# Grouping the small score products of two attentions, summing squares four tiles at a time, and a new order

## The chip, the core and the metric

The kernel runs on one core of a Trainium2 chip. A core has TensorE (PE, matrix products; its weight loads, PEld, overlap them), VectorE (DVE), ScalarE (ACT), GpSimd (POOL), the queue of SyncE (SP) that starts the transfers, and 16 DMA engines. Each engine works through its own instruction list in the order in which it was written. The metric is the device time of one execution in microseconds (us), here the median of timed runs; the profile shows one execution.

## The reference, cut to what matters

256 tokens of width 1024, in float32, with 16 learned meta tokens put ahead of them (T = 272 rows), go through four layers. Shortened:

```python
# layer 0 and 1, each: h = h + rmsnorm(mix(rmsnorm(h))); h = h + rmsnorm(conv_ffn(rmsnorm(h)))
# mix of layer 0, forgetting attention, 16 heads of 64
s = einsum('bhqd,bhkd->bhqk', q, k) * scale + c_q[..., :, None] - c_k[..., None, :]
o = softmax(where(causal, s, NEG)) @ v * sigmoid(og)
# mix of layer 1, gated DeltaNet, 8 heads of 128
dec = exp(where(incl, gc[..., :, None] - gc[..., None, :], -inf))
A, qk = (k @ k.T) * dec * beta, (q @ k.T) * dec
...
# conv_ffn
gate, up = split(causal_dwconv(h @ w_up, conv_w)); return (gelu(gate) * up) @ w_down
# then, without the meta tokens: MLA (16 heads), layer_norm, MoBA (16 heads of 64), layer_norm
```

With 256 tokens and blocks of 256, MoBA has one block, so it is causal attention with rotated queries and keys, times silu of a gate.

## The kernel before, in words

**A recorder and a planner.** The kernel is written once in program order, but nothing is emitted at once: `Rec.add` records each operation, with an estimated cost from `_cost` and the operations it depends on, under the name of a part (`ameta`, `att3`, `dout0`, `bq2`). Operations inside a `bundle` become one entry and stay together. `Rec.order` then plays the engines against each other: it always takes the operation that can start first, and between those that can start together the one with the lowest rank, which is the place in program order minus numbers of the table `SHIFT` for the part and for the part on one engine. It models PE's clock (`PeClock`), the DMA of the weights (three constants) and the places in the buffer pools. Where it foresees a gap of PE of 400 ns or more, `keep_warm` fills it with products of a mask that nobody reads (tile `idle`, line L449). All other instructions are issued from one line, L498, so the profile tells them apart by tile names.

**Weights.** Each MB of weights comes as one fp32 tile `raw` through SP's queue into one of two buffers; ACT writes its rounded part `wh`, DVE the rest `wl`, and PE adds three products per tile of 128 rows: `wh` with `xh`, `wl` with `xh`, `wh` with `xl`. Activations lie transposed, as tiles of 128 features by up to 272 tokens. The accumulators are PSUM banks: tag `psm` for projections, at most 5 at a time, `psx` for everything else, at most 6.

**Norms.** `rstd` (L914) multiplies each square tile `sq` by a full 128x128 matrix of ones (`const` in the rows) into one bank, so that every row of the bank holds the sum over features, and `ln_exp` makes `rstd` of it. `sq_rstd` (L922) does so for the 6 tiles of MLA's query latent; `pre` (L931), the norm ahead of a projection, for 8 tiles, one at a time, as each residual tile becomes ready.

**Scores of the forgetting attention.** `attend` (L1108) treats the 256 tokens; the 16 meta tokens as queries are treated in `meta` (L1158): per head a 16x16 block gets the score product (`km`, `qm`), the decay of the keys (one row of the table `crow`, picked by a one-hot column `oh`) and the causal mask (`causb` times the unit matrix `identb`).

**DeltaNet.** `dn_scores` (L1374) runs four times, for the keys and the queries of two groups of four heads. It adds mask and decay into one bank (`pe`) and the product into another (`pk`); first for the 16 meta rows of four heads, then for two blocks of 128 tokens per head. The code is, for the second:

```python
for c in range(2):
    with nc.bundle():
        nc.tensor.matmul(pe[:, s], self.identb, mask, start=True, stop=False)
        nc.tensor.matmul(pe[:, s], oh[:, h:h + 1].to_broadcast([96, P]), rows[:, a:b], start=False, stop=True)
        nc.tensor.matmul(pk[:, s], k[:, 4 * g + h, a:b], x[:, 4 * g + h, a:b], start=True, stop=True)
```

**A product in column strips.** `narrow` (L866), the projection to 16 gate logits, multiplies four weight tiles of 32 columns into four strips of 32 rows of one bank, in one bundle.

**MoBA.** `rope64` (L1702) makes the rotated queries `bq` of two heads from a projection through ACT copies and three DVE operations; `causal_pairs` (L1647) multiplies them with the keys `bk`, 2 heads and 2 query blocks at a time, four products in one bundle.

## Time and profile before

| | |
|---|---|
| timed runs | 1137.41, 1146.93, 1147.97 us; median 1146.93 |
| profiled execution | 1139.0 us, its span 1137.2 |
| mean granted clock of PE | 0.989 |
| busy, of the span | PE 96%, PEld 91%, DVE 73%, ACT 60%, POOL 1% |
| DMA | 159.05 MB, mean 140 GB/s |
| instructions | PE 9064 products, DVE 1847, ACT 1372 |

PE's busy time counts overlapping products once, and a product's row carries the time from its start until its result is out, so neighbours overlap: the distance of two starts is what one costs PE. A row "a <- b, c" names the tile written and the tiles read. "x2" behind an fp32 product of small tiles is one product in two passes.

### The profile page before, as it was taken

Reading aid. Unit: us, or ns where it says so; the run is one execution under the profiler, and the core shown is the slowest. Engines: PE = TensorE matmul, PEld = TensorE weight load, DVE = VectorE, ACT = ScalarE, POOL = GpSimd, SP = SyncE. Lnnn points to the kernel's source line nnn. Section 1 sums busy time; section 2 is a strip of 40 time slices with the busy share of each in tenths; the row PEclk is TensorE's granted clock in tenths of the full one; section 3 lists DMA queues with packets and bytes.
Section 4 is the critical chain, followed back from the end, with each engine's and each line's share of the span. In section 5 each row is a group of like instructions: output and inputs, shape, how many; then the busy total and the mean of one; then the engine's idle time right before and its main releaser. Section 6 shows DMA issues by size and latency. Waiting matters only on the chain.

```text
span 1137.2 us, 22513 instructions
## 1 busy us (share of the span) xinstructions
PE 1095.8 (96%) x9064; PEld 1031.4 (91%) x9064; DVE 828.8 (73%) x1847; ACT 684.5 (60%) x1372; POOL 10.3 (1%) x85
## 2 busy tenths in 40 slices
PE   7999999999999989999999999999999999999897
PEld 6998889899999978888889899999989988999887
DVE  5678774798876577899755789986475667856686
ACT  4567655665655465554686656565355589556881
POOL 0000000000000000000000000000000000000000
PEclk9999989999999999999999999999999999999999
DMA  7552323354645543234122345655545452466331
GB/s 222 169 161 82 112 75 112 112 189 153 198 157 169 177 148 112 75 112 140 49 75 75 112 149 193 204 188 189 175 146 169 131 172 75 149 194 206 120 112 38
DMA packets 153359, 159.05 MB, mean 140 GB/s; under 512 B 5989, under 2 KB 151062, under 8 KB 153254
## 3 DMA queue, kind: packets, MB, share of 16 engines
q1 hardware_dynamic: 153254, 157.61, 43.7%
q8 instruction: 71, 1.16, 0.4%
q14 instruction: 34, 0.28, 0.1%
HBM read 156.55 MB, written 1.05 MB: 139 GB/s over the span
## 4 chain that ended last, share of the span: by engine, by line
PE 57%; DVE 14%; DMA 14%; ACT 12%; issue 3%; SPq 0%; DVEq 0%; ACTq 0%
PE psm L498 46%; PE psx L498 10%; DVE wl L498 6%; DMA raw<-in_ffn_w_up_dram 5%; ACT wh L498 5%; DMA raw<-in_mla_w_in_dram 2%; ACT rx L498 2%; DMA raw<-in_dn_w_in_dram 2%; DVE y L498 2%; ACT e L498 1%; DMA raw<-in_moba_w_kv_dram 1%; DVE t L498 1%; DMA masks<-in_const_dram 1%; DMA raw<-in_mla_w_uq_dram 1%; DMA xt<-in_x_dram 1%
## 5 line engine op out<-in xcount | busy, mean ns | idle before, releaser
L498 DVE TENSOR_TENSOR wl<-raw,wh 128x1024 fp32r<-128x1024 f32 (+1 forms) x297 | 350.2, 1192 | 149.5 <-ACT wh L498 101.0
L498 PE MATMUL psm<-xh,wh 128*128 128x272 f32 (+4 forms) x1544 | 452.7, 293 | 0.4 <-ACT wh L498 0.4
L498 PE MATMUL psm<-xh,wl 128*128 128x272 f32 (+4 forms) x1544 | 443.3, 287 | 7.7 <-DVE wl L498 7.6
L498 PE MATMUL psm<-xl,wh 128*128 128x272 f32 (+4 forms) x1544 | 441.9, 286 | 0.1
L498 ACT ACTIVATE wh<-raw 128x1024 fp32r<-128x1024 f32 (+1 forms) x296 | 298.9, 1032 | 185.3 <-PE psm L498 57.8
L498 PEld LDWEIGHTS psm<-xh,wl 128*128 128x128 f32 (+1 forms) x1544 | 291.8, 189 | 12.4 <-DVE wl L498 11.2
L498 PEld LDWEIGHTS psm<-xh,wh 128*128 128x128 f32 (+1 forms) x1544 | 291.7, 189 | 6.9 <-issue 3.1
L498 PEld LDWEIGHTS psm<-xl,wh 128*128 128x128 f32 (+1 forms) x1544 | 291.6, 189 | 0.9 <-DVE xl L498 0.9
L498 PE MATMUL psm<-al,wh 128*128 128x272 f32 (+1 forms) x352 | 100.3, 285 | 0.0
L498 PE MATMUL psm<-ah,wh 128*128 128x272 f32 (+1 forms) x352 | 100.2, 285 | 0.0
L498 PE MATMUL psm<-ah,wl 128*128 128x272 f32 (+1 forms) x352 | 100.0, 284 | 0.0
L498 DVE SCALAR_TENSOR_TENSOR y<-uc,cols,y 128x272 f32<-128x272 f32 (+1 forms) x176 | 81.8, 487 | 6.3 <-ACT y L498 5.3
L498 PEld LDWEIGHTS psm<-ah,wl 128*128 128x128 f32 x352 | 66.3, 188 | 0.0
L498 PEld LDWEIGHTS psm<-al,wh 128*128 128x128 f32 x352 | 66.3, 188 | 0.0
L498 PEld LDWEIGHTS psm<-ah,wh 128*128 128x128 f32 x352 | 66.2, 188 | 0.0
L498 ACT ACTIVATE y<-uc,cols 128x272 f32<-128x272 f32 (+1 forms) x88 | 43.5, 508 | 37.0 <-DVE uc L498 36.9
L498 DVE TENSOR_TENSOR uc<-psm,rstd 128x272 f32<-128x272 f32 (+2 forms) x112 | 47.0, 427 | 8.6 <-PE psm L498 6.2
L498 ACT ACTIVATE e<-e,mx 128x256 f32<-128x256 f32 (+3 forms) x96 | 43.0, 450 | 10.1 <-DVE mx L498 10.0
L498 PE MATMUL psx<-sq,const 128*128 128x272 f32 (+4 forms) x144 | 41.2, 398 | 6.5 <-ACT sq L498 2.9
L498 PEld LDWEIGHTS psx<-sq,const 128*128 128x128 f32 (+1 forms) x144 | 20.5, 166 | 15.0 <-ACT sq L498 7.3
L498 DVE CUSTOM_DVE_ANT_0 e<-psx,causal 128x256 f32<-128x256 f32 (+3 forms) x96 | 30.1, 356 | 4.7 <-PE psx L498 4.5
L498 ACT ACTIVATE sq<-psm 128x272 f32<-128x272 f32 (+2 forms) x40 | 15.1, 384 | 27.2 <-PE psm L498 27.1
(350 smaller groups left out, 1777.9 us busy)
## 6 DMA issues: line engine op xcount, KB each, us to landing
raw<-in_ffn_w_up_dram SPq DMA_DIRECT2D x44, 1024.0 KB, 5.2
raw<-in_attn_w_in_dram SPq DMA_DIRECT2D x16, 1024.0 KB, 5.6
raw<-in_ffn_w_down_dram SPq DMA_DIRECT2D x16, 1024.0 KB, 4.9
raw<-in_dn_w_in_dram SPq DMA_DIRECT2D x16, 1024.0 KB, 6.2
raw<-in_mla_w_in_dram SPq DMA_DIRECT2D x8, 1024.0 KB, 5.5
raw<-in_moba_w_kv_dram SPq DMA_DIRECT2D x8, 1024.0 KB
raw<-in_moba_w_in_dram SPq DMA_DIRECT2D x8, 1024.0 KB, 5.4
raw<-in_ffn_w_down_dram SPq DMA_DIRECT2D x8, 768.0 KB
```

Source lines behind the costliest of these rows:

```text
L498: return getattr(real, method)(*(_real(a) for a in args), **{k: _real(v) for k, v in kw.items()})
```

## The change

Four things change in the code. `pre` and the long form of `sq_rstd` collect squares and multiply four of them at once by 32 columns of ones into four strips of 32 rows (`sums4`); a new `rstd4` copies the bank to SBUF on ACT (tile `s4`) and sums over the strips with one product of full ones, whose result is 32 times the sum. `meta` puts the key decays of all heads on the diagonal of a tile `mrow` with two DVE operations, adds them and the masks to two banks with one wide product each (`oneb` is a tile of ones), and then makes 16 score products of one shape, the two heads of a pair alternating between the banks. `dn_scores` does the same for its meta rows, and for its blocks adds mask and decay 256 columns wide, one bundle per head. The planner gets other costs: for products side by side (`BESIDE`), for transfers, for transposes, and for how many columns keep the clock up; and every number of `SHIFT` is new.

```diff
@@ -209,13 +209,13 @@
...
-    TICK, ENOUGH = 10240 / 3, 2900
+    TICK, ENOUGH = 10240 / 3, 3300
 
...
+BESIDE = {(64, 128): 2, (128, 64): 2, (32, 64): 2, (64, 64): 2, (128, 32): 4, (32, 32): 2}
+
+DMA_HEAD, DMA_TAIL, DMA_RATE = 1100.0, 950.0, 310.0
...
             elif op.last[:2] != tiling[:2]:
                 cost += DRAIN
-            elif op.last != tiling:
-
-                cost *= 0.52
+            if tiling[:2] in BESIDE and op.last is not None and op.last[:2] == tiling[:2] and (
+                    tiling not in op.beside and len(op.beside) < BESIDE[tiling[:2]]):
+
+                cost *= 0.05
+                op.cols -= cols if tiling[:2] != (64, 64) else 0.0
+                op.beside.append(tiling)
+            else:
+                op.beside = [tiling]
             op.last = tiling
         op.cost += cost
         op.nbytes += nbytes
@@ -396,8 +405,8 @@
                 self.keep_warm(clock["PE"], start, pe, free, result)
             if o.engine == "SP":
                 clock["SP"] = start + 475
-                dma = max(dma, start + 1100) + o.nbytes / 360.0
-                o.finish = dma + 890
+                dma = max(dma, start + DMA_HEAD) + o.nbytes / DMA_RATE
+                o.finish = dma + DMA_TAIL
             else:
                 cost = o.cost
                 if o.engine == "PE":
...
-SHIFT = {"ameta": 35, ("ameta", "PE"): 165, ("ameta", "DVE"): -70, ("ameta", "ACT"): -180, "aog0": 50, ("aog0",
...
+SHIFT = {"ameta": 90, ("ameta", "PE"): -110, ("ameta", "DVE"): -110, ("ameta", "ACT"): 10, "aog0": -145, ("aog0",
...
@@ -803,9 +818,11 @@
         self.bd64 = self.const_t("bd64r", [P, P], FR)
         nc.vector.tensor_copy(self.bd64, masks[:, 3 * P:])
 
-        self.oh = self.const_t("oh", [96, 32], BF)
+        self.oh = self.const_t("oh", [96, 48], BF)
+        self.oneb = self.oh[:, 32:]
+        nc.gpsimd.memset(self.oneb, 1.0)
         for i in range(3):
-            nc.vector.tensor_copy(self.oh[32 * i:32 * i + 32], self.ident[:32, :32])
+            nc.vector.tensor_copy(self.oh[32 * i:32 * i + 32, :32], self.ident[:32, :32])
 
 
     def act(self, out, in_, func, **kw):
@@ -921,7 +938,29 @@
 
     def sq_rstd(self, tiles, n, n_feat, eps=None):
 
-        return self.rstd([self.square(t, n) for t in tiles], n, n_feat, eps)
+        sq = [self.square(t, n) for t in tiles]
+        if len(sq) <= 4:
+            return self.rstd(sq, n, n_feat, eps)
+        nc, p = self.nc, self.ax_ps()
+        with nc.bundle():
+            for i, a in enumerate(sq):
+                j = 32 * (i % 4)
+                nc.tensor.matmul(p[j:j + 32, :n], self.ones[:, :32], a, start=i < 4, stop=i + 4 >= len(sq))
+        return self.rstd4(p, n, n_feat)
+
+    def sums4(self, p, sq, n, first, last):
+
+        with self.nc.bundle():
+            for j, a in enumerate(sq):
+                self.nc.tensor.matmul(p[32 * j:32 * j + 32, :n], self.ones[:, :32], a, start=first, stop=last)
+
+    def rstd4(self, p, n, n_feat):
+
+        s = self.work([P, n], label="s4")
+        self.nc.scalar.activation(s, p[:, :n], AF.Copy)
+        r = self.ax_ps()
+        self.nc.tensor.matmul(r[:, :n], self.ones, s, start=True, stop=True)
+        return self.ln_exp(r[:, :n], 32 * n_feat)
 
     def square(self, src, n):
         s = self.work([P, n], label="sq")
@@ -935,7 +974,7 @@
         nc = self.nc
         n = T - n0
         xh, xl = self.slab_t(dt=FR, label="xh"), self.slab_t(dt=FR, label="xl")
-        p = self.ax_ps()
+        p, sq = self.ax_ps(), []
 
         def tile(k):
             g = self.col(gname, 8 * l + k)
@@ -945,9 +984,11 @@
             else:
                 nc.scalar.activation(xh[:, k, n0:], h, AF.Copy, scale=g)
             nc.vector.scalar_tensor_tensor(xl[:, k, n0:], h, g, xh[:, k, n0:], op0=OP.mult, op1=OP.subtract)
-            nc.tensor.matmul(p[:, :n], self.ones, self.square(h, n), start=k == 0, stop=k == KT - 1)
-
-        return tile, lambda: ((xh, xl), self.ln_exp(p[:, :n], D))
+            sq.append(self.square(h, n))
+            if k % 4 == 3:
+                self.sums4(p, sq[-4:], n, k == 3, k == KT - 1)
+
+        return tile, lambda: ((xh, xl), self.rstd4(p, n, D))
 
     def out_proj(self, name, units, xs, gname, l, n0, nxt):
 
@@ -1158,20 +1199,30 @@
         def meta():
             nc.at("ameta")
 
+            mrow = self.work([96, 2, 8, META], BF, label="mrow")
+            ohs = oh[:, :16].rearrange("r (p h) -> r h p", h=2)
+            for h in range(2):
+                nc.vector.tensor_tensor(mrow[:, h], ohs[:, h].unsqueeze(2).to_broadcast([96, 8, META]),
+                                        crow[:, :META].unsqueeze(1).to_broadcast([96, 8, META]), op=OP.mult)
+
             sm = self.work([META, 2, 8, META], label="smeta")
             mx = self.work([META, 2, 8], label="mmx")
+            banks = [self.ax_ps() for _ in range(2)]
+            with nc.bundle():
+
+                for h in range(2):
+                    nc.tensor.matmul(banks[h][:META, :P], self.oneb, mrow[:, h], start=True, stop=False)
+                for h in range(2):
+                    nc.tensor.matmul(banks[h][:META, :P], self.identb[:META, :META],
+                                     self.causb[:META, :META].unsqueeze(1).to_broadcast([META, 8, META]),
+                                     start=False, stop=False)
+                for pr in range(8):
+                    for h in range(2):
+                        hp = slice(64 * h, 64 * h + 64)
+                        nc.tensor.matmul(banks[h][:META, META * pr:META * pr + META], qm[hp, pr], km[hp, pr],
+                                         start=False, stop=pr == 7)
             for h in range(2):
-                ps = self.ax_ps()
-                hp = slice(64 * h, 64 * h + 64)
-                with nc.bundle():
-                    for pr in range(8):
-                        cs = slice(META * pr, META * pr + META)
-                        nc.tensor.matmul(ps[:META, cs], qm[hp, pr], km[hp, pr], start=True, stop=False)
-                        nc.tensor.matmul(ps[:META, cs], oh[:, 2 * pr + h:2 * pr + h + 1].to_broadcast([96, META]),
-                                         crow[:, :META], start=False, stop=False)
-                        nc.tensor.matmul(ps[:META, cs], self.identb[:META, :META], self.causb[:META, :META],
-                                         start=False, stop=True)
-                psv = ps[:META, :P].rearrange("p (h k) -> p h k", h=8)
+                psv = banks[h][:META, :P].rearrange("p (h k) -> p h k", h=8)
                 nc.vector.tensor_reduce(mx[:, h], psv, axis=AX.X, op=OP.max)
                 nc.vector.tensor_tensor(sm[:, h], psv, mx[:, h].unsqueeze(2).to_broadcast([META, 8, META]),
                                         op=OP.subtract)
@@ -1377,13 +1428,16 @@
         pe, pk = self.ax_ps(), self.ax_ps()
         n0 = 0 if x is k else N0
         m = META - n0
+        mrow = self.work([96, 4, m], BF, label="mrow")
+        nc.vector.tensor_tensor(mrow, oh[:, :4].unsqueeze(2).to_broadcast([96, 4, m]),
+                                rows[:, n0:META].unsqueeze(1).to_broadcast([96, 4, m]), op=OP.mult)
         with nc.bundle():
+            nc.tensor.matmul(pe[:META, :4 * m], self.oneb, mrow, start=True, stop=False)
+            nc.tensor.matmul(pe[:META, :4 * m], self.identb[:META, :META],
+                             mask[:META, n0:META].unsqueeze(1).to_broadcast([META, 4, m]), start=False, stop=True)
             for h in range(4):
-                s = slice(m * h, m * h + m)
-                nc.tensor.matmul(pe[:META, s], self.identb[:META, :META], mask[:META, n0:META], start=True, stop=False)
-                nc.tensor.matmul(pe[:META, s], oh[:, h:h + 1].to_broadcast([96, META]), rows[:, n0:META], start=False,
+                nc.tensor.matmul(pk[:META, m * h:m * h + m], k[:, 4 * g + h, :META], x[:, 4 * g + h, n0:META], start=True,
                                  stop=True)
-                nc.tensor.matmul(pk[:META, s], k[:, 4 * g + h, :META], x[:, 4 * g + h, n0:META], start=True, stop=True)
         em = self.work([META, 4, m], label="em")
         v3 = lambda p: p[:META, :4 * m].rearrange("p (h i) -> p h i", h=4)
         nc.vector.tensor_tensor(em, v3(pe), cb[:META, 0].unsqueeze(2).to_broadcast([META, 4, m]), op=OP.add)
@@ -1391,13 +1445,17 @@
         last = nc.vector.tensor_tensor(em, em, v3(pk), op=OP.mult)
         for h in range(4):
             pe, pk, e = self.ax_ps(), self.ax_ps(), self.work([P, 256], label="dE")
+            with nc.bundle():
+                nc.tensor.matmul(pe[:, :2 * P], self.identb, mask.unsqueeze(1).to_broadcast([P, 2, P]), start=True,
+                                 stop=False)
+                nc.tensor.matmul(pe[:, :2 * P], oh[:, h:h + 1].to_broadcast([96, P]), rows[:, META:T], start=False,
+                                 stop=True)
+                for c in range(2):
+                    a, b = TT[1 + c]
+                    nc.tensor.matmul(pk[:, P * c:P * c + P], k[:, 4 * g + h, a:b], x[:, 4 * g + h, a:b], start=True,
+                                     stop=True)
             for c in range(2):
-                a, b = TT[1 + c]
                 s = slice(P * c, P * c + P)
-                with nc.bundle():
-                    nc.tensor.matmul(pe[:, s], self.identb, mask, start=True, stop=False)
-                    nc.tensor.matmul(pe[:, s], oh[:, h:h + 1].to_broadcast([96, P]), rows[:, a:b], start=False, stop=True)
-                    nc.tensor.matmul(pk[:, s], k[:, 4 * g + h, a:b], x[:, 4 * g + h, a:b], start=True, stop=True)
                 self.act(e[:, s], pe[:, s], AF.Exp, bias=cb[:, 1 + c, h:h + 1])
             v2 = lambda p: p[:, :256].rearrange("p (c i) -> p c i", c=2)
             nc.vector.tensor_tensor(out[:, 2 * h:2 * h + 2], v2(pk), v2(e), op=OP.mult)
```

Line L498 of before is line L507 of the changed kernel. How the order moves on PE is shown at three places, each before and after the change.

First, the meta scores of the forgetting attention, in `ameta`, on PE; `psx_2138` and `psx_2140` are the banks of the last pair of heads ahead of them. Before:

```order
L498 MATMUL psx_2138<-q_373_2029,q_366_1985 128x144
L498 MATMUL psx_2140<-q_373_2029,q_366_1985 128x144
L498 MATMUL psx_2149<-km_970,qm_968 16x16
L498 LDWEIGHTS oh_240
L498 MATMUL psx_2149<-crow_211,oh_240 16x16
L498 LDWEIGHTS identb_236
L498 MATMUL psx_2149<-causal_165,identb_236 16x16
L498 MATMUL psx_2149<-km_970,qm_968 16x16
```

After, behind three transposes of the pair ahead (`psx_2147`):

```order
L507 MATMUL psx_2147<-const_174,e_2102 128x128 x2
L507 LDWEIGHTS oh_217
L507 MATMUL psx_2155<-mrow_1992,oh_217 16x128
L507 LDWEIGHTS oh_217
L507 MATMUL psx_2157<-mrow_1992,oh_217 16x128
L507 LDWEIGHTS identb_253
L507 MATMUL psx_2155<-causal_165,identb_253 16x128
L507 LDWEIGHTS identb_253
L507 MATMUL psx_2157<-causal_165,identb_253 16x128
L507 MATMUL psx_2155<-km_892,qm_862 16x16
L507 MATMUL psx_2157<-km_892,qm_862 16x16
L507 MATMUL psx_2155<-km_892,qm_862 16x16
```

The triple of score, decay and mask stood 16 times in a row, over two banks; now four wide products stand first and 16 score products behind them, the bank changing each time.

Second, the norm behind the attention output on PE: the squares `sq` of the new residual tiles, and the first projections of the feed-forward layer (`psm`). Before:

```order
L449 LDWEIGHTS causal_165
L449 MATMUL idle_2610<-causal_165 128x256
L498 MATMUL psx_2641<-sq_2635,const_174 128x272
L498 MATMUL psx_2641<-sq_2645,const_174 128x272
L498 MATMUL psm_2653<-xh_2639,wh_2481 128x272
L498 MATMUL psm_2653<-xh_2639,wl_2492 128x272
L498 MATMUL psm_2653<-xl_2647,wh_2481 128x272
```

After:

```order
L507 MATMUL psm_2685<-xh_2636,wh_2461 128x272
L507 MATMUL psm_2685<-xh_2636,wl_2493 128x272
L507 MATMUL psm_2685<-xl_2642,wh_2461 128x272
L507 MATMUL psx_2696<-sq_2640,const_174 32x272
L507 MATMUL psx_2696<-sq_2646,const_174 32x272
L507 MATMUL psx_2696<-sq_2660,const_174 32x272
L507 MATMUL psx_2696<-sq_2680,const_174 32x272
L507 MATMUL psm_2662<-xh_2636,wh_2433 128x272
```

Two full products of squares stood behind the idle ones and ahead of the first projection; now a group of four strips stands behind 18 projection products.

Third, MoBA's last scores on PE (`bk`, `bq`), in `causal_pairs`; `psm_13516` and `psm_13429` are projections of the last part. Before:

```order
L498 MATMUL psx_13478<-bk_12600,bq_12751 128x256
L498 MATMUL psx_13480<-bk_12600,bq_12751 128x256
L498 MATMUL psx_13478<-bk_12600,bq_12751 128x128
L498 MATMUL psx_13480<-bk_12600,bq_12751 128x128
L498 MATMUL psx_13495<-bk_12600,bq_12751 128x256
L498 MATMUL psx_13497<-bk_12600,bq_12751 128x256
L498 MATMUL psx_13495<-bk_12600,bq_12751 128x128
L498 MATMUL psx_13497<-bk_12600,bq_12751 128x128
L498 MATMUL psx_13510<-const_174,e_13471 128x128
L498 MATMUL psx_13510<-const_174,e_13469 128x128 x2
L498 MATMUL psm_13516<-xh_12291,wh_12991 128x256
```

After:

```order
L507 MATMUL psx_13404<-bk_12662,bq_12808 128x256
L507 MATMUL psx_13406<-bk_12662,bq_12808 128x256
L507 MATMUL psx_13404<-bk_12662,bq_12808 128x128
L507 MATMUL psx_13406<-bk_12662,bq_12808 128x128
L507 MATMUL psx_13412<-bk_12662,bq_12808 128x256
L507 MATMUL psx_13414<-bk_12662,bq_12808 128x256
L507 MATMUL psx_13412<-bk_12662,bq_12808 128x128
L507 MATMUL psx_13414<-bk_12662,bq_12808 128x128
L507 MATMUL psm_13429<-wh_13377,xh_12262 128x256
L507 MATMUL psm_13429<-wl_13401,xh_12262 128x256
```

Four pairs of heads stood in one run, of which the last two are shown; now three do, and projections follow at once.

## Rows read from the trace of the kernel before

**Rows 1.** Page, part 1: busy us, share of span, instructions.

```profile
PE 1095.8 (96%) x9064; PEld 1031.4 (91%) x9064; DVE 828.8 (73%) x1847; ACT 684.5 (60%) x1372; POOL 10.3 (1%) x85
```

**Rows 2.** Page, part 4: the chain that ended last, by engine.

```profile
PE 57%; DVE 14%; DMA 14%; ACT 12%; issue 3%; SPq 0%; DVEq 0%; ACTq 0%
```

**Rows 3.** Timeline of PE, first norm: start, us, engine, line, operation, tiles, forms.

```profile
25.60 1.54 PE L498 MATMUL psx<-sq,const 128*128 128x272 f32 x6
26.97 0.27 PE L498 MATMUL psx<-const,rows 128*128 128x128 f32 x1
```

**Rows 4.** Timeline of PE, `narrow`: two groups of four strips among projections.

```profile
423.78 0.29 PE L498 MATMUL psm<-xh,wl 128*128 128x272 f32 x1
423.90 0.29 PE L498 MATMUL psm<-xl,wh 128*128 128x272 f32 x1
424.12 1.12 PE L498 MATMUL psm<-H,nw 128*32 128x272 f32 x16
425.17 0.39 PE L498 MATMUL psm<-xh,wh 128*128 128x272 f32 x1
```

**Rows 5.** Timeline of PE, norm behind the attention output; in brackets idle before, releaser.

```profile
198.92 1.58 PE L449 MATMUL idle<-causal 128*128 128x256 bf16 x13
201.76 1.46 PE L498 MATMUL psx<-sq,const 128*128 128x272 f32 x4 [1.26 <-ACT sq L498]
202.86 0.49 PE L498 MATMUL psm<-xh,wh 128*128 128x272 f32 x1
```

**Rows 6.** Timeline of PE, `meta`: first triple of 16, and what follows them.

```profile
157.09 0.21 PE L498 MATMUL psx<-km,qm 64*16 64x16 f32 x2
157.24 0.18 PE L498 MATMUL psx<-crow,oh 96*16 96x16 bf16 x1
...
162.83 0.81 PE L498 MATMUL psx<-const,v 128*16 128x128 f32 x3
```

**Rows 7.** Windows: length, busy PE, PEld, DVE, ACT, POOL; clock, DMA share, GB/s.

```profile
158.00:174.00 16.00, 16.00 (x155) 11.71 (x155) 9.33 (x30) 4.97 (x15) 0.00 (x0) 0.68 0.01 1
```

**Rows 8.** Timeline of PE, `meta`: values of 16 heads, 32 passes.

```profile
170.85 1.17 PE L498 MATMUL psx<-pTm,vm 16*64 16x16 f32 x32
```

**Rows 9.** Timeline of PE, `dn_scores`, meta rows: first of four triples, what follows.

```profile
457.31 0.17 PE L498 MATMUL psx<-masks,identb 16*16 16x16 bf16 x1
...
458.37 0.39 PE L498 MATMUL psm<-xh,wh 128*128 128x272 f32 x1
```

**Rows 10.** Timeline of PE, `dn_scores`, blocks: one triple and the next one's start.

```profile
461.50 0.23 PE L498 MATMUL psx<-masks,identb 128*128 128x128 bf16 x1
461.56 0.22 PE L498 MATMUL psx<-grow,oh 96*128 96x128 bf16 x1
...
461.90 0.22 PE L498 MATMUL psx<-masks,identb 128*128 128x128 bf16 x1
```

**Rows 11.** Timeline of PE, DeltaNet's scan: fp32 products of 128 columns, two passes each.

```profile
593.06 0.39 PE L498 MATMUL psm<-dq,T 128*128 128x128 f32 x2
593.29 0.39 PE L498 MATMUL psm<-QK,dU 128*128 128x128 f32 x2
```

**Rows 12.** Windows, keys' half of `dn_scores`.

```profile
460.00:520.00 60.00, 57.28 (x638) 53.44 (x637) 56.98 (x188) 35.01 (x62) 0.80 (x7) 1.00 0.35 104
```

**Rows 13.** Waits of PE: us in total, times, longest.

```profile
PE psm L498 <- DVE wl L498: 8.4, 16, 0.9
PE psx L498 <- DVE bq L498: 4.0, 3, 2.1
```

**Rows 14.** Windows, MoBA's last part.

```profile
1076.00:1086.00 10.00, 6.15 (x36) 5.30 (x37) 7.77 (x28) 9.46 (x28) 0.00 (x0) 0.66 0.07 25
```

**Rows 15.** Page, part 6: weight loads, size, median us to landing.

```profile
raw<-in_ffn_w_up_dram SPq DMA_DIRECT2D x44, 1024.0 KB, 5.2
```

**Rows 16.** Groups by form, ACT: busy, mean ns, idle before with its releaser.

```profile
L498 ACT ACTIVATE sq<-psm 128x272 f32<-128x272 f32 x16 | 6.1, 390 | 13.4 <-PE psm L498 13.4
```

**Rows 17.** Tile `em`, DVE: ns least/median/most, first to last start, forms.

```profile
L498 DVE TENSOR_TENSOR em<-psx,tab x4: 147/178/205, 459.4 to 562.1; 16x64 f32<-16x64 f32 x2, 16x8 f32<-16x8 f32 x2
```

More of the change, by code (lines that the diff above doesn't have):

```diff
@@ L211 @@
     __slots__ = ("engine", "cost", "deps", "rank", "calls", "bufs", "finish", "nbytes", "users", "wait", "ready", "seq",
-                 "cols", "tail", "prio", "part", "first", "last")
+                 "cols", "tail", "prio", "part", "first", "last", "beside")
 class PeClock:
-    TICK, ENOUGH = 10240 / 3, 2900
+    TICK, ENOUGH = 10240 / 3, 3300
     def __init__(self):
@@ L293, in add @@
             op.calls, op.bufs, op.finish, op.nbytes, op.users = [], [], None, 0, []
-            op.seq, op.cols, op.first, op.last = len(self.ops), 0.0, None, None
+            op.seq, op.cols, op.first, op.last, op.beside = len(self.ops), 0.0, None, None, []
             self.ops.append(op)
@@ L527, in _cost @@
             cost = max(0.4535 * n + 2.6, 108) if dt == FR else max(n / 2.4 + 3 + (8 if rows == 96 else 0), 28)
-        return cost, n * (1 if method == "transpose" else passes) * rows / P, tiling
+        return cost, n * passes * rows / P, tiling
     if engine == "DVE":
```

10 lines of the change are left out of this document (5 added, 5 removed), and 232 rows, old and new, of the table SHIFT.

## The prediction

> **What bounds the kernel now.** I read the page first, then the chain of waits, the timeline of TensorE (PE below), the windows with the granted clock, and the waits. PE is busy for 1095.8 of 1137.2 us [rows 1]; the chain that ends last runs on PE for 57% of the span, and the rest of it is handed round between VectorE (DVE), DMA and ScalarE (ACT) [rows 2]. So PE is the first limit: work taken from it comes off the end wherever PE has more work waiting, and comes off nothing where PE stands waiting anyway. Outside the large projections PE has three kinds of stretch that this change touches: full-array sums of squares, long runs of tiny products, and a run at half clock.
>
> The profiled execution took 1139.0 us (span 1137.2 and 1.8 around it). The three timed runs gave 1137.41, 1146.93 and 1147.97, so the median stands 7.9 us above the execution that I read rows from. The sum below is made against 1139.0.
>
> **Sums of squares.** By the order of both, 38 full products of a square tile with `ones` leave (24 of 272 columns, 8 of 258, 6 of 256); in their place stand 10 groups of up to four 32-row products and 5 closing full products. Three full products of 272 take 26.97 - 25.60 = 1.37 us, 0.46 each [rows 3]; I use that for all widths. A group of four in column strips is already in the kernel: `narrow`. Two such groups start at 424.12 and PE goes on at 425.17; the projection before them would have been through at 424.02 (423.90 and the 0.12 between neighbours, 423.78 to 423.90) [rows 4]. That is 1.15 us for two, so four run side by side in about the time of one, and some 0.2 of it is the change of array shape before and after. A group that stands alone pays both changes: 0.46 + 0.20 = 0.66. Sum: 38 x 0.46 = 17.5 leave, 10 x 0.66 + 5 x 0.46 = 8.9 come, 8.6 us less PE work. Not all of it is on the path: behind the attention output PE waits 1.26 us for the first square and only then, after two such products, starts the next projection [rows 5]. Two products at each of three such norms (2.8 us) cost nothing before. I take 5.8; bounds 3 and 8.6.
>
> The closing step adds a copy on ACT (nearest row 0.39 [rows 16]), a product (0.46) and two hand-overs before `rstd`. What waits for `rstd` is the evacuation of the projections; PE can fill five PSUM banks first, each with 24 products of 0.12 us [rows 4], 14 us in all. I cost it at nothing; without that cover it is about 1.2 us at each of five places.
>
> **Small products of the meta tokens (`meta`).** Now 16 triples of score, decay and mask run from 157.09 to 162.83, 5.74 us; a product and the change of shape behind it take 0.15 [rows 6]. After, four bf16 products of 128 columns (0.06 each [rows 10]) come first and then 16 score products of one shape with heads alternating. The 16 products of `pTm` with `vm`, of like size and in alternating strips, took 1.17 us [rows 8], of which some 0.15 is the tail of the last. With the changes of shape: 0.24 + 1.0 + 0.3 = 1.5. At 0.15 each they would be 16 x 0.15 + 0.24 + 0.2 = 2.8; at half the row's time, 1.0. I take the first, nearest in form: 4.2 us less, bounds 2.9 and 4.7. The Trainium skill, TensorEngine Tiling (Array Packing), section Instruction Overhead, speaks against this size: a small product costs some 60 cycles whatever its width. By it (an estimate from that page: 60 cycles at 2.4 GHz, 25 ns) dropping 28 of 48 products would save only 0.7 us. The row has 5.74 us for 48, 0.12 each, because every one follows another shape, so the row decides.
>
> **Clock.** From 158 to 174 us the mean granted clock is 0.68 [rows 7]. It fell from 2.4 to 1.2 GHz within the run of tiny products and came back before its end. 16 x 0.32 = 5.1 us lost. With the run cut to about 1.5 us I expect it mostly kept, but the stretch behind it still consists of transposes and 16-row products. I take two thirds, 3.4; bounds 0 and 5.1. The Trainium skill (TensorE: Matmul & The Clock Gate, section Part 1: The HAM clock gate) says that low activity throttles and dense activity releases; it cannot say on which side this stretch falls.
>
> **Decay products of DeltaNet (`dn_scores`), four calls.** The four meta triples take 458.37 - 457.31 = 1.06 us [rows 9]; after, two bf16 and four fp32 products of one shape, about 0.6: 0.46 x 4 = 1.8. The large triples take 0.40 each, a pair 0.80 [rows 10]; after, two fp32 products at 0.23 [rows 11] and two bf16 of double width at 0.12, 0.70: 0.10 x 16 = 1.6. The keys' half of this 3.4 lies where DVE is busy for 57.0 of 60 us [rows 12] and sets the pace, so it brings nothing. New there are the DVE products for `mrow`, two for the keys, priced by the nearest small operation at 0.18 [rows 17]: 0.4 on that path. The two of `meta` and the two of the queries are hidden beside PE. Net 1.7 - 0.4 = 1.3; bounds -0.4 and 3.4.
>
> **New order.** Here the trace has no price for most places; one can be read. In MoBA's last part PE waits 4.0 us for `bq` in three waits [rows 13], and from 1076 to 1086 has only 6.15 us busy at a mean clock of 0.66 [rows 14]: 4.0 + 6.15 x 0.34 = 6.1 us to be had. Before, the scores of four pairs stand in one run there; now three, with 24 projection products ahead of the next, and most `bq` are made earlier. `bq` is still made through DVE behind the last projection, so I take 3.5; bounds 0 and 6.1. The waits for `wl` (8.4 us in 16 [rows 13]) may go or grow: the planner's 1 MB load goes from about 4.9 to 5.4 us, the trace has a median of 5.2 [rows 15], as far from one as from the other; I take 0, bounds -10 and +4. The 32 additional idle products (0.12 each) stand in waits at the start and at four norms; where thirteen stood before, PE still idled 1.26 us [rows 5], which holds nine more. Nothing; 3.8 us if no wait is left.
>
> **Sum.** 5.8 + 4.2 + 3.4 + 1.3 + 3.5 = 18.2; 1139.0 - 18.2 = 1120.8. I forecast 1121, 2.3% below the median of 1146.93.
>
> **Rivals.** (a) *The splits pace it.* If only the share of the chain that is PE's, 57% [rows 2], of the 18.2 comes through and PE waits for `wl` instead, 10.4 are left: 1129; with the 7.9 by which the median stands above the profiled execution, 1137. For it: the DVE-bound stretch. Against: `wl` costs PE only 8.4 us now. (b) *The strips don't run side by side*, because the four squares come one by one. Then groups cost what single products did and 5.8 is lost: 1127. Against: [rows 4]. (c) *The clock falls anyway*, in the transposes behind the meta scores: 3.4 lost, 1124. For it: the stretch stays poor in columns; the rule of the clock gate allows it. (d) *Slower: the group of four blocks PE's queue.* PE takes its queue in order, and in the order a group stands ahead of projections. ACT makes a square and an `xh` per tile; at 0.39 for one such pass [rows 16] that is 0.8 us, so the fourth square comes some 2.4 us after the first. If PE reached each of the 10 groups at its first square, 24 us of waiting, and 1.2 at each of five closings, come on top: 1121 + 30 = 1151, 0.4% over the median. From about 2.0 us per group (1147) it is slower. Against: the groups stand behind 18 to 24 projection products. (e) *All comes*: 8.6 + 4.7 + 5.1 + 3.4 + 6.1 + 4 = 32, 1107.
>
> **How the numbers follow.** Forecast (1112 to 1127, its own range) 0.50, (a) 0.20, (b) 0.06, (c) 0.11, (d) 0.04, (e) 0.09. The range leaves out less than 2 in 10: 1106 to 1139. A measurement of this kernel can tell about 1%; faster by over 1% means below 1135.5. The forecast, (b), (c), (e) and most of (a) lie there: 0.84 faster, 0.12 within 1%, 0.04 slower.
>
> **What would show it.** Each step has its mark: four 32-row products starting within 0.05 us and a group through in 0.7 us; the 16 meta scores through in 1.0 to 1.3 us; the granted clock between 155 and 175 us at 0.9 or more; PE's wait for `bq` under 2 us in all; PE's wait for squares at a norm not above the 1.26 us of now [rows 5]. Wrong would be: PE waits for `sq` of several us at the groups, waits for `wl` well over 8.4 us, or DVE rather than PE at the head of the chain.

## The result and the profile after

The changed kernel took 1105.13 us (median of 4, 1103.73 to 1108.97) against 1146.31 before (1137.41 to 1147.97): ratio 0.9661, 95% interval 0.9606 to 0.9717, so 3.4% faster. The profiled execution took 1105.2 us, its span 1103.3: 33.9 us less span than before, where the forecast's sum was 18.2. The median lies just under the low end of the range, 1106.

The page of the changed kernel, part 1 (busy us, share, instructions) and part 4 (chain that ended last), answering [rows 1, 2]:

```profile
PE 1076.4 (98%) x9022; PEld 1014.8 (92%) x9022; DVE 825.0 (75%) x1853; ACT 685.7 (62%) x1377; POOL 10.2 (1%) x86
```

```profile
PE 75%; DVE 11%; ACT 7%; DMA 4%; issue 2%; SPq 0%; DVEq 0%; ACTq 0%
```

PE lost 19.4 us of busy time, but the span lost 33.9: the other 14.5 us are time in which PE stood. The chain says the same: DMA had 14% of it and has 4%. PE's waits (us in total, times, longest), answering [rows 13]:

```profile
PE psm L507 <- ACT xh L507: 3.4, 3, 1.3
...
PE psx L507 <- DVE bq L507: 0.6, 1, 0.6
PE psx L507 <- ACT sq L507: 0.5, 2, 0.3
...
PE psm L507 <- DVE wl L507: 0.2, 1, 0.2
```

The waits for `wl` (8.4 us before) and for `bq` (4.0) are nearly gone. To see where all 33.9 us come from I summed, for each product of PE, the distance from its start to the next one's start, by kind of product; waits and slow clock lie inside the kinds. This is worked out from the traces, in us; "half" is the time at 1.2 GHz that the trace lists, from the start on and to some 2 us behind the end of the span:

```
                     span   projections squares meta decay  bq   idle other edges | half
before              1137.2     908.9     31.4   5.7  18.5  12.0  17.8 134.4  8.5  | 26.1
changed             1103.3     892.5     23.0   0.9  17.1   7.6  19.8 134.2  8.2  | 19.1
changed, once more  1099.5     891.4     22.9   0.9  15.4   7.6  20.0 133.0  8.2  |  9.5
```

"projections" holds all products into banks of the tag `psm`, "squares" also the closing products, "decay" masks, decays and the key products beside them. The largest fall, 16.4 us, is in the projections, whose products the change did not touch; 14.6 of it are in those that read `wh` or `wl`.

### The profile page after: what moved, and what is told of

It reads as the page before. It is cut to its first block, busy times and chain, and to the rows that moved or that the text cites. A ratio compares the mean times of both kernels' runs of the same rounds, so it can differ in the third digit from the quotient of the medians.

```text
span 1103.3 us, 22442 instructions
## 1 busy us (share of the span) xinstructions
PE 1076.4 (98%) x9022; PEld 1014.8 (92%) x9022; DVE 825.0 (75%) x1853; ACT 685.7 (62%) x1377; POOL 10.2 (1%) x86
## 4 chain that ended last, share of the span: by engine, by line
PE 75%; DVE 11%; ACT 7%; DMA 4%; issue 2%; SPq 0%; DVEq 0%; ACTq 0%
PE psm L507 64%; PE psx L507 11%; DVE wl L507 3%; ACT wh L507 2%; DVE t L507 1%; DMA raw<-in_mla_w_in_dram 1%; ACT rx L507 1%; DVE y L507 1%; ACT e L507 1%; DMA xt<-in_x_dram 1%; DMA raw<-in_ffn_w_up_dram 1%; DMA raw<-in_mla_w_uq_dram 1%; DVE dv L507 1%; DVE dq L507 1%; DMA raw<-in_dn_w_in_dram 1%
## 5 line engine op out<-in xcount | busy, mean ns | idle before, releaser
L507 DVE TENSOR_TENSOR wl<-raw,wh 128x1024 fp32r<-128x1024 f32 (+1 forms) x297 | 349.5, 1192 | 141.2 <-PE psm L507 71.4
L507 PE MATMUL psm<-xh,wh 128*128 128x272 f32 (+3 forms) x1544 | 449.2, 291 | 3.4 <-ACT xh L507 3.4
L507 PE MATMUL psm<-xh,wl 128*128 128x272 f32 (+3 forms) x1544 | 441.5, 286 | 0.4 <-DVE wl L507 0.2
L507 PE MATMUL psm<-xl,wh 128*128 128x272 f32 (+3 forms) x1544 | 441.1, 286 | 0.5 <-DVE xl L507 0.4
L507 ACT ACTIVATE wh<-raw 128x1024 fp32r<-128x1024 f32 (+1 forms) x296 | 297.4, 1030 | 161.1 <-PE psm L507 89.4
L507 PEld LDWEIGHTS psm<-xh,wh 128*128 128x128 f32 x1544 | 291.2, 189 | 12.4 <-issue 5.8
L507 PEld LDWEIGHTS psm<-xh,wl 128*128 128x128 f32 x1544 | 291.4, 189 | 2.2 <-DVE wl L507 1.9
L507 PEld LDWEIGHTS psm<-xl,wh 128*128 128x128 f32 x1544 | 291.2, 189 | 1.3 <-DVE xl L507 1.1
L507 PE MATMUL psm<-ah,wh 128*128 128x272 f32 (+1 forms) x352 | 100.3, 285 | 0.0
L507 PE MATMUL psm<-al,wh 128*128 128x272 f32 (+1 forms) x352 | 100.2, 285 | 0.0
L507 PE MATMUL psm<-ah,wl 128*128 128x272 f32 (+1 forms) x352 | 99.9, 284 | 0.0
L507 DVE SCALAR_TENSOR_TENSOR y<-uc,cols,y 128x272 f32<-128x272 f32 (+1 forms) x176 | 81.9, 488 | 8.5 <-ACT y L507 7.5
L507 PEld LDWEIGHTS psm<-ah,wl 128*128 128x128 f32 x352 | 66.3, 188 | 0.0
L507 ACT ACTIVATE y<-uc,cols 128x272 f32<-128x272 f32 (+1 forms) x88 | 43.9, 510 | 36.1 <-DVE uc L507 35.7
L507 PEld LDWEIGHTS psm<-al,wh 128*128 128x128 f32 x352 | 66.3, 188 | 0.0
L507 PEld LDWEIGHTS psm<-ah,wh 128*128 128x128 f32 x352 | 66.2, 188 | 0.0
L507 DVE TENSOR_TENSOR uc<-psm,rstd 128x272 f32<-128x272 f32 (+2 forms) x112 | 47.1, 427 | 4.9 <-PE psm L507 2.9
L507 ACT ACTIVATE e<-e,mx 128x256 f32<-128x256 f32 (+3 forms) x96 | 42.9, 451 | 5.4 <-DVE mx L507 5.4
L507 ACT ACTIVATE rx<-psm 32x256 f32<-32x256 f32 (+1 forms) x69 | 25.9, 376 | 9.5 <-DVE rt L507 7.8
L507 DVE CUSTOM_DVE_ANT_0 e<-psx,causal 128x256 f32<-128x256 f32 (+2 forms) x96 | 30.2, 356 | 1.9 <-PE psx L507 1.9
L507 PE MATMUL psx<-const,e 128*128 128x128 f32 (+1 forms) x176 | 28.0, 278 | 1.9 <-DVE e L507 1.0
L507 ACT ACTIVATE y<-y 128x272 f32<-128x272 f32 (+1 forms) x44 | 18.4, 417 | 17.7 <-DVE y L507 17.6
```

The source lines that it names most:

```text
L507: return getattr(real, method)(*(_real(a) for a in args), **{k: _real(v) for k, v in kw.items()})
```

## The experiments

**Products and order apart.** For the first four runs the changed kernel is planned as it is; then, in PE's entries, the calls are exchanged for others, so that ACT, DVE and SP keep their lists row for row:

```diff
+    @contextmanager
+    def instead(self):
+        self.sink = []
+        yield
+        self.ops[-1].calls, self.sink = self.sink, None
```

The first puts all old products in the places of the new ones; copies, closing products and `mrow` stay (the triples stand in it as before, and `dn_scores` is treated like `meta`). The next three runs take one of these three parts each:

```diff
+        with self.nc.instead():
+            for j, a in enumerate(sq):
+                self.nc.tensor.matmul(p[:, :n], self.ones, a, start=first and j == 0, stop=last and j == 3)
...
-        return self.ln_exp(r[:, :n], 32 * n_feat)
+        return self.ln_exp(r[:, :n], 128 * n_feat)
...
+            with nc.instead():
+                for h in range(2):
+                    ps, hp = banks[h], slice(64 * h, 64 * h + 64)
+                    for pr in range(8):
+                        cs = slice(META * pr, META * pr + META)
+                        nc.tensor.matmul(ps[:META, cs], qm[hp, pr], km[hp, pr], start=True, stop=False)
...
```

> The changed kernel with its planned order kept entry for entry on every engine, but in PE's list the old products stand in the places of the new ones: 38 full products of squares for the 10 groups of strips, 16 triples in the meta scores, triples in the decay products of DeltaNet (the copies, the closing products and mrow stay). In the profiled executions the change took 34 us, 1139.0 to 1105. Theory A, order: the prediction's 14.7 us for products and clock (5.8 + 4.2 + 3.4 + 1.3) were about right and the missing 16 us come from the new order, which keeps wl ahead of PE. Then this takes 1105 + 15 = 1120 us (1115 to 1125), PE's waits for wl stay under 2 us and those for bq under 1 us. Theory B, products: the products were worth more than costed, since the lighter PE is what removed the waits. Then most of the 34 us come back, 1130 to 1139, and the waits for wl return to 5 us or more.

It took 1123.49 us, ratio 0.983 (0.9788 to 0.9871); span 1121.7, projections 891.4, `bq` 7.6. Its waits of PE:

```profile
PE psm L516 <- DVE wl L516: 0.9, 3, 0.5
```

Theory A holds: with all the old products the new order still keeps `wl` ahead of PE. Of the 33.9 us of span 15.5 belong to the order (1137.2 to 1121.7) and 18.4 to the products; by medians 18.3 belong to the order (1141.82, the kernel before beside it, to 1123.49) and 18.4 to the products.

> Order kept; only the squares are full products again, 38 for the 10 groups; copies and closing products stay. PE work: 38 x 0.45 = 17.1 us for 10 x 0.57 = 5.7 of now, 11.4 more. Theory A (all of it is on the path, as PE is now the head of the chain for 75%): 1105 + 11 = 1116. Theory of the prediction (some 2.8 us of it fill waits at norms): 1105 + 8.6 = 1113.5. Theory C (strips do nothing, their gain is in the order): within 3 us of 1105.

1113.87 us, ratio 0.9746 (0.97 to 0.9793). Squares cost PE 34.0 in place of 23.0 us, 11.0 more, near the 11.4 reckoned; the span grew by 8.6, the median by 8.7, or by 10.5 against the later executions of the changed kernel (1103.33, below). So 0.5 to 2.4 us of the 11.0 are hidden: the first median speaks for the prediction's theory (1113.5), the second for theory A, and C is out. The closing products stay in this run, so its 8.6 is not the 8.6 of the prediction, in which they are counted.

> Order kept; only the meta scores are 16 triples again in the place of the two wide pairs and 16 scores. Products alone cost 5.74 us before and about 1 us now: at least 4.2 us more. Theory A: the granted clock behind it falls for 10.2 us as before, in place of 3.4 now, another 3.4 us: 1105 + 4.5 + 3.4 = 1113. Theory B: the clock does not depend on these products, 3.4 us at half clock stay: 1105 + 4.5 = 1109.5.

1108.18 us, ratio 0.9695 (0.9652 to 0.9739). The meta products cost 5.8 in place of 0.9 us, and the median rose by 3 to 5 us. The time spoke for theory B, though it can't tell the clock: the time at 1.2 GHz differs as much between executions of one kernel (last section). The traces of all runs together say more of it (below, "Clock").

> Order kept; only the decay products of DeltaNet are triples again in the places of the grouped ones; mrow stays on DVE. PE work 4 x 0.46 + 16 x 0.10 = 3.4 us more. Theory A (PE sets the pace there now): 1105 + 3.4 = 1108.4. Theory of the prediction (DVE sets the pace in the keys' half): 1105 + 1.7 = 1106.7. Theory C: it changes whether the clock falls at 537 and 568 us, where the changed kernel has 3.4 us at half clock each; without these falls the sum is 1105 + 3.4 - 3.4 = 1105.

1105.44 us, ratio 0.9676 (0.9634 to 0.9718), the same as the changed kernel's. Its four executions lie between 1103.8 and 1108.9, too wide to tell 1.7 from 3.4 or 0 us: inconclusive on the time. By start distances the kind "decay" is 20.4 us against 17.1, slow clock included. Theory C's ground did not come: this profiled execution falls to 1.2 GHz there too, for 6.8 us at 538 and 3.4 at 572.

One by one the three parts add 12.1 us to the median of 1105.13, or 17.5 to that of 1103.33; all together they added 18.4, or 20.2. Some 3 to 6 us are in no single part.

**Why the order mattered.** The next question was what the old order lost. One theory was late loads:

```diff
         self.nc.sync.dma_start(raw, w[r0:r0 + kt * P, c0:c0 + n].rearrange("(k p) n -> p k n", p=P))
+        self.loads = getattr(self, "loads", 0) + 1
+        if self.loads > 4 and kt == KT:
+            with self.nc.instead():
+                self.nc.gpsimd.memset(raw[:, 6:], 0.0)
+                self.nc.sync.dma_start(raw[:, :6], w[r0:r0 + 6 * P, c0:c0 + n].rearrange("(k p) n -> p k n", p=P))
```

> The kernel before, order kept; each weight load of eight row tiles (from the fifth load on) brings six of them, 768 in place of 1024 KB, and the other two are set to zero by GpSimd: a quarter of most weights is left out of the computation. The split, the products and their order are as before. Theory T (transfers: before, the loads landed later than its plan reckoned, so that splits stood in ACT's and DVE's lists ahead of their data): a load lands some 0.8 us sooner, PE's waits for wl fall from 8.4 to 2 us or less, ACT's waits for raw from some 115 us to 60 or less, and the time falls by 6 to 12 us, to 1127 to 1133. Theory O (the place of the splits in the lists of ACT and DVE, whatever the loads do): the waits for wl stay at 6 to 9 us and the time within 3 us of 1139.

1124.51 us where the kernel before beside it had 1140.96, ratio 0.987 (0.9813 to 0.9927). Its page, part 4, and its waits of PE:

```profile
PE 80%; DVE 9%; ACT 6%; DMA 3%; issue 2%; SPq 0%; DVEq 0%; POOL 0%; ACTq 0%; POOLq 0%
```

```profile
PE psx L507 <- DVE bq L507: 4.3, 3, 2.1
PE psx L507 <- ACT sq L507: 4.1, 3, 1.6
PE psm L507 <- DVE wl L507: 3.9, 8, 0.9
```

With most of its loads a quarter smaller, the old order with the old products has DMA at 3% of the chain in place of 14%; projections fall from 908.9 to 895.9 us. It takes about what the new order takes with the old products (1123.49). The waits named `wl` halve only, to 3.9, not to 2 or less, and ACT's waits for `raw` fall from 123.5 to 75.6, not to 60 or less; yet the time falls by 16.4 us, more than the 6 to 12 of theory T: the row for `wl` does not hold all that late loads cost. The wait for `bq` stays (4.3), so that one has another cause.

```diff
-                dma = max(dma, start + 1100) + o.nbytes / 360.0
+                dma = max(dma, start + 1100) + o.nbytes / 310.0
```

> The kernel before, planned anew with one constant of the change, the transfer rate of 310 in place of 360 (the table of before, the old products). Theory T: the splits now stand where their data has landed; waits for wl fall to 4 us or less and the time to 1128 to 1134. Theory O: the table was made for the old constants; waits for wl stay at 6 us or more, and others may come, 1137 to 1150.

1146.09 us, ratio 1.0036 (1.0001 to 1.007): no gain. Its waits of PE:

```profile
PE psx L498 <- ACT sq L498: 5.9, 3, 2.9
PE psm L498 <- DVE wl L498: 3.6, 8, 0.8
PE psx L498 <- DVE sq L498: 3.1, 4, 1.6
```

The mark of theory T came (waits for `wl` 8.4 to 3.6), its time did not: waits for squares rose to 9.0 from 4.8, and the time at 1.2 GHz to 42.0 from 26.1 us. So a constant nearer to the measured loads is not enough in the old table; whether a table made with it would do is not shown.

```diff
-AHEAD = 400
+AHEAD = 410
```

> The kernel before, planned anew with a bound of the planner that has nothing to do with transfers (how far an entry may run ahead of the next one's buffer: 410 in place of 400): a control, of how much any new order of the old products moves. Theory T: waits for wl stay at 6 to 10 us, time within 5 us of 1139. Theory O: as likely better as worse, waits for wl anywhere between 2 and 14 us.

1143.42 us, ratio 1.0033 (1.0 to 1.0066), waits for `wl` 6.0: within what theory T allowed, and one measure for how little an arbitrary new order brings.

The next run makes loads land in halves:

```diff
+        if n == 256:
+            with self.nc.instead():
+                for o in (0, P):
+                    self.nc.sync.dma_start(raw[:, :, o:o + P],
+                                           w[r0:r0 + kt * P, c0 + o:c0 + o + P].rearrange("(k p) n -> p k n", p=P))
```

> The changed kernel, order kept; each weight load of 256 columns is issued as two of 128 columns for the same buffer, so that pieces of 512 bytes take the place of pieces of 1024 and the load lands later (how much, this run shows). Theory T: the new order has slack against late loads only as far as its constants reckon, some 0.5 us per load; landing 1 us later brings the waits for wl back, 5 us or more, and 1112 or more. Theory O: the splits stand far enough behind; waits for wl under 2 us and within 3 us of 1105, as long as the queue keeps up.

1101.71 us, ratio 0.9671 (0.9615 to 0.9727). It was meant to land later and did the opposite where it counts: a split waits only for its own half, and ACT's waits for `raw` fell from 66.5 us (sum of their rows) to 30.7. So it could not test the slack; the same edit on the kernel before could test lateness without leaving anything out.

> The kernel before, order kept; each weight load of 256 columns is issued as two of 128 columns, as in the run on the changed kernel, where ACT's waits for raw fell from some 66 to some 29 us. The bytes are those of before. Theory L (the late loads of the old order are what the new order removed; with a quarter of the bytes left out the old order took 1124): the first half lands sooner, ACT's waits for raw fall from some 125 us to 60 or less, the waits for wl from 8.4 to 4 or less, and the time to 1124 to 1131. Theory M (only the bytes count, not when the first of them land): within 4 us of 1141.

1133.97 us against 1142.44 beside it, ratio 0.9939 (0.9916 to 0.9963). ACT's waits for `raw` fell from 123.5 to 68.0 us, those of PE for `wl` to 3.8. The direction is theory L's, the size half of the 16.4 us that the smaller loads brought: neither 60 us of waits nor 1124 to 1131 was reached. The profiled execution has 41.8 us at 1.2 GHz, where before has 26.1, which may hide part of the gain.

> The changed kernel, order kept, with a quarter of most weights left out of the loads (and of the computation), as in the run on the kernel before, which gained 16 us by it. Theory L: the new order has removed the lateness already, so there is nothing more to gain: within 4 us of 1105. Theory N (the new order only moved the waits to other places, and loads still pace it): 1095 or less.

1102.04 us, ratio 0.9658 (0.9633 to 0.9684), its chain 1% DMA. In the old order smaller loads bring 16 us, in the new one 1 to 3: theory L, the new order has lost nearly all of the lateness.

> The changed kernel itself once more, as the measure for the next run: 1103.5 to 1109, median 1105.

1103.33 us (1100.4 to 1105.08) where the kernel before beside it had 1142.44, ratio 0.9669 (0.9644 to 0.9694): the result holds.

> The changed kernel with every weight load of 256 columns issued as two of 128. Its first four executions took 1100.8 to 1103.1 us where those of the changed kernel took 1103.7 to 1109.0. If earlier first halves help, 1100 to 1103.5 again and 2 to 4 us under the run before it in this list; if that was chance (where the clock fell), the two medians lie within 1.5 us.

1103.14 us, ratio 0.9668 (0.9645 to 0.9691). The lead of halved loads over the changed kernel was chance: 0.2 us side by side. No run is faster than the changed kernel by more than its spread.

**Open.** Whether the table or the planner's constants made the order good can't be divided: for the new table with the old transfer constants, for the old table in the changed kernel and for the new table in the kernel before, the planner runs out of free buffers before it has an order, so none of these could be run. And in the waits of the old order I did not follow single loads.

## Why the prediction was right in direction and short in size

The sum, term by term, against the two profiled executions (us saved):

| step | predicted (bounds) | measured |
|---|---|---|
| squares | 5.8 (3 to 8.6) | 8.4 |
| meta products | 4.2 (2.9 to 4.7) | 4.8 |
| decay products | 1.3 (-0.4 to 3.4) | 1.4 |
| `bq` | 3.5 (0 to 6.1) | 4.4 |
| clock, 158 to 174 | 3.4 (0 to 5.1) | 3.4 there, as much lost elsewhere |
| `wl`, on projections | 0 (-10 to +4) | 16.4 |
| idle products | 0 (-3.8 to 0) | -2.0 |
| all else | | 0.5 |

The measured column adds up to 33.9; the clock lies inside the kinds. It is PE's time by start distances, not the share of the path. By the first run, the 15.7 us that the sum fell short by divide into 12.0 of the order (15.5 where I had 3.5) and 3.7 of products and clock (18.4 where I had 14.7).

**Squares: mechanism and price right.** A norm of the changed kernel on PE's timeline (start, us, tiles; in brackets idle before):

```profile
188.74 2.57 PE L458 MATMUL idle<-causal 128*128 128x256 bf16 x22
192.37 0.39 PE L507 MATMUL psm<-xh,wh 128*128 128x272 f32 x1 [1.07 <-ACT xh L507]
...
195.70 0.29 PE L507 MATMUL psm<-xl,wh 128*128 128x272 f32 x1
195.92 0.67 PE L507 MATMUL psx<-sq,const 128*32 128x272 f32 x8
196.51 0.39 PE L507 MATMUL psm<-xh,wh 128*128 128x272 f32 x1
```

From the end of the projection's share (195.70 + 0.13) to the next one a group costs 0.68; forecast 0.66. I took 2.8 us off because two squares at three norms filled waits; by the second run 0.5 to 2.4 us are hidden. At the norm shown, a projection now stands where the squares filled the wait: it waits 1.07 us for `xh`, where the square had waited 1.26 [rows 5]. That this is why less is hidden is argued, not shown. Rival (d), a group that blocks PE, is refuted: all waits of PE for squares are 0.8 us (0.5 on ACT, 0.3 on DVE). The closing step, costed at nothing, shows on ACT, whose waits for sums ahead of `rstd` rose from 7.4 to 16.1 us, but PE waits ahead of none of the five closing products, and each cost it 0.26 at most where I had 0.46; no run took the step away.

**Meta products: right, a little small** (4.8, just over the upper bound of 4.7). The same stretch after the change, answering [rows 6]:

```profile
151.95 0.28 PE L507 MATMUL psx<-mrow,oh 96*16 96x128 bf16 x2
152.16 0.28 PE L507 MATMUL psx<-causal,identb 16*16 16x128 bf16 x2
152.36 0.57 PE L507 MATMUL psx<-km,qm 64*16 64x16 f32 x32
152.86 0.93 PE L507 MATMUL psx<-const,e 128*16 128x128 f32 x7
```

0.91 us for all, against 5.74; I had 1.5. The 16 scores take 0.50, half of the nearest row's [rows 8]. In the trace the passes start in pairs: each half of the array's rows starts one every 0.025 us (152.400, 152.425, 152.450 and so on), the other half 0.007 behind. In the triples a product behind one of another shape started 0.10 us after it (157.133, 157.236, 157.342, 157.444); that price went with the triples. The trace agrees with the 25 ns estimated from the Trainium skill's rule (TensorEngine Tiling (Array Packing), Instruction Overhead) for a pass in one half, but the 0.7 us saved that were estimated with it stand against 4.8, since the rule has no price for the change of shape.

**Decay products.** An answer to [rows 10]:

```profile
443.50 0.28 PE L507 MATMUL psx<-masks,identb 128*128 128x256 bf16 x1
443.62 0.27 PE L507 MATMUL psx<-grow,oh 96*128 96x256 bf16 x1
443.73 0.61 PE L507 MATMUL psx<-dk 128*128 128x128 f32 x4
444.18 0.27 PE L507 MATMUL psx<-masks,identb 128*128 128x256 bf16 x1
```

0.68 us per head where 0.70 was forecast. The sum hit (1.4) partly by chance: in the second profiled execution, without a fall of the clock there, the kind is 15.4 us, 3.1 less than before.

**Clock: right for the triples, too small over many executions.** The window from 158 to 174 us (columns as in [rows 7]) in the changed kernel, in the changed kernel once more, and in the kernel before with smaller loads:

```profile
158.00:174.00 16.00, 16.00 (x154) 14.82 (x154) 6.29 (x13) 5.58 (x11) 0.00 (x0) 0.89 0.21 68
```

```profile
158.00:174.00 16.00, 16.00 (x166) 14.81 (x165) 6.54 (x15) 5.58 (x11) 0.00 (x0) 1.00 0.21 68
```

```profile
158.00:174.00 16.00, 16.00 (x172) 12.98 (x171) 9.16 (x27) 5.41 (x13) 0.00 (x0) 0.89 0.00 1
```

0.68 became 0.89, 3.4 us, as forecast. (In the kernel before the clock came back at 171.0 us, well behind the last triple, and not before the end of the run.) The third row has the old triples and the same 0.89, so one execution each can't show that the triples made the difference; fourteen profiled executions can, in the main. From 150 to 185 us the granted clock is 0.76 to 0.95 in the seven with triples (the kernel before 0.85, its four variants 0.95, 0.80, 0.76 and 0.85, the first and the third run 0.90 each) and 0.95 or 1.00 in the seven without. With order and loads alike it is 0.90 twice with triples, and 0.95 and three times 1.00 without; here the third run, which has the triples, and the changed kernel once more:

```profile
150.00:185.00 35.00, 35.00 (x319) 30.16 (x318) 18.43 (x56) 15.05 (x38) 0.00 (x0) 0.90 0.21 66
```

```profile
150.00:185.00 35.00, 34.18 (x338) 30.79 (x337) 21.49 (x58) 17.98 (x43) 0.00 (x0) 1.00 0.35 114
```

The changed kernel's first profiled execution lost as much at a place where before had nothing, 530 to 575 us, and not in its second execution:

```profile
530.00:575.00 45.00, 43.86 (x411) 40.00 (x407) 27.94 (x66) 32.50 (x83) 0.20 (x2) 0.92 0.21 68
```

```profile
530.00:575.00 45.00, 43.91 (x426) 40.08 (x424) 29.75 (x72) 34.71 (x92) 0.20 (x2) 1.00 0.20 66
```

The one pair of profiled executions shows little of the clock. For every timed run the record has the mean granted clock; one minus it, times the span, is an estimate of what the slow clock cost. In 39 executions of the kernel before (0.978 to 0.991) that is 10 to 25 us, in the median 17; in ten of the changed kernel (0.990 to 0.997) 3 to 11, in the median 7. So some 10 us of the 37 between the two medians (1141.82 and 1104.58) go with the clock, of which I had 3.4 and a part of `bq`; and the execution that I read rows from (0.989) was one of the kernel before with little slow clock.

**`bq`: right.** The waits fell from 4.0 to 0.6 us (a wait of 0.7 for the keys `bk` is new), and from 1040 to 1052 the granted clock is full, where [rows 14] had 0.66.

```profile
1040.00:1052.00 12.00, 9.69 (x80) 8.55 (x79) 9.14 (x30) 11.18 (x28) 0.00 (x0) 1.00 0.28 89
```

**The step that failed: "The waits for `wl` may go or grow".** I took 0 with at most 4 to gain; 16.4 us came off the projections. Three things went wrong in it. First, the price to be had was read from PE's row for `wl` alone, 8.4, and even that was cut to 4, while the chain [rows 2] gave 14% to DMA. The row counts only the idle time between the end of one product's row and the next start. By start distances, worked out from the traces, the 16 products ahead of these waits cost 11.7 us more than 16 neighbours at 0.126; in the changed kernel one such product is left and costs 0.3 more. So 11.4 of the 16.4 us lie right at the waits for `wl`. Second, lateness was judged by one median, 5.2 us [rows 15], which I called as far from 4.9 as from 5.4; it is 0.3 over the first and 0.2 under the second. The page has other loads beside it, and most are slower:

```profile
raw<-in_attn_w_in_dram SPq DMA_DIRECT2D x16, 1024.0 KB, 5.6
raw<-in_ffn_w_down_dram SPq DMA_DIRECT2D x16, 1024.0 KB, 4.9
raw<-in_dn_w_in_dram SPq DMA_DIRECT2D x16, 1024.0 KB, 6.2
raw<-in_mla_w_in_dram SPq DMA_DIRECT2D x8, 1024.0 KB, 5.5
```

Third, I left out who waits for the loads first. These are ACT's waits in the kernel before, its four largest for `raw`; all of them add up to 123.5 us in 74 waits:

```profile
ACT wh L498 <- DMA raw<-in_ffn_w_up_dram: 26.6, 21, 5.9
ACT wh L498 <- DMA raw<-in_ffn_w_down_dram: 24.3, 17, 3.8
ACT wh L498 <- DMA raw<-in_attn_w_in_dram: 21.7, 7, 6.0
ACT wh L498 <- DMA raw<-in_dn_w_in_dram: 21.3, 8, 6.9
```

ACT takes its list in order, so what stands behind such a split (squares, evacuations, gates) is late too, and PE's wait then carries another name; this is argued, and the row for squares does not bear it out: with smaller loads PE's waits for them are 4.3 us, where they were 4.8. In the changed kernel ACT's waits for `raw` add up to 66.5 in 44. They are no price either: the halved loads took some 30 us off them there, and nothing off the time. Case (e) came out in size, 32 us, but only in part for its reasons: decay products brought 1.4 where it had 3.4, and the loads 16.4 where it had 4.

**Idle products.** 32 more cost PE 2.0 us by start distances, part of it waits in which they stand. No run took them away, so what they give or cost stays open.

## What to carry to other kernels

When a change reorders everything, price the order too: read the chain's share of DMA and the waits of the engine that receives the loads, not only the waits of the busiest engine. They bound what is to be had and do not price it: here ACT's waits fell from 123.5 to 66.5 us, and the order brought 15.5 to 18.3. Making loads cheaper while the order is kept shows in one run how much an order loses to them. An order can be kept word for word while products are exchanged in it, and that divides a change which a replanning would mix.

## What the runs showed of the hardware that was not expected

Where PE falls to 1.2 GHz differs between executions of one program. The changed kernel's two profiled executions have 19.1 and 9.5 us at that clock and spans of 1103.3 and 1099.5: half of 9.6 is 4.8 us, and 3.8 of it are seen. So differences of up to some 5 us between single executions of the changed kernel need not come from the edit, which is why the decay products' and the halved loads' effects could not be told from four executions each. The 39 executions of the kernel before lie further apart, from 1132.11 to 1149.27 us, and the slower ones have in the main the lower mean granted clock. The Trainium skill (TensorE: Matmul & The Clock Gate, Part 1: The HAM clock gate) ties the clock to what PE did before; the traces agree in that the fall near 161 us stands behind small products, but the same instruction list fell to 1.2 GHz between 530 and 575 us in one execution and not in the next.

Loads in pieces of 512 bytes instead of 1024 cost the kernel no time here: 1103.14 against 1103.33 us, with ACT waiting 35.6 us for `raw` instead of 65.2. They do cost the transfers time: the packets took 52.4% of the 16 engines' span instead of 45.3%, so where loads set the pace it could come out otherwise.
